# The attention stage's list of operations written anew, its last output tiles in single banks, and the next weight sum's load behind it

## The chip, the core and the metric

The kernel runs on one core of a Trainium2 chip. The metric is the time of one execution in microseconds of the device: the median of three runs is 1532.93 us (1531.55, 1532.93 and 1534.12).

The core has these engines: PE (matrix products), PEld (its weight loads, which lie beside the products), DVE, ACT and POOL (elementwise work), and SP, which mainly issues transfers. Each goes through its own list of instructions in order and waits on semaphores for the others. PE's accumulators lie in PSUM, in eight banks.

## The reference, cut to what matters

One inference step of a decoder with two layers, for 512 prompt tokens and 8 sample tokens that share the weights. The change lies in the second layer's attention (16 heads of 64, 4 key heads, a window of 128 tokens, a sink logit for each head) and ends where that layer's second feed-forward begins:

```python
q = _rope((h @ w_q[j]).reshape(B, T, N_KV_HEADS, GROUP, HEAD_DIM), pos)
out = _window_attention(q, kk, vv, wb, pos0, attn_sinks[j]) @ w_o[j]
x = x + out
x = x + 0.5 * _swiglu(_rmsnorm(x, norm_g[l, 2]), ...)

# in _window_attention, per block of 128 queries and its 256 keys
s = q @ k * HEAD_DIM ** -0.5;  s = where(mask, s, -inf)
m = max(max(s), sink);  p = exp(s - m)
denom = sum(p) + exp(sink - m)
out = (p / denom) @ v
```

## The kernel before, in words

Everything runs with the model dimension (1024, as 8 tiles of 128) on the partitions and the 520 tokens along the free axis, in two halves of 260 columns. Each float32 operand is split into a high and a low part, and a product is three matmuls (high by high, low by high, high by low): one k step of one output tile is 6 matmuls of 260 columns (`mm`, L883). For weights the high part is an ACT copy (`wh`, L450, or L421 where the queue of weights makes it) and the low part a DVE subtraction (`wl`, L454 or L425), for a chunk of 4 k steps at a time. `wh` and `wl` have six buffers.

The attention stage is all of `yoco_step` from L1937 to the next feed-forward. PSUM is there two "duos" of two banks, for products that are 520 columns wide and for scores, and four single banks, for transposes and values. The stages of a query tile t (two heads) are: eight query steps on PE (`q_step`), an ACT copy out of PSUM (`q_evac`, L1964, `qraw`); transfers that gather the rotary rows of a group of tiles (`q_gather`, L1972; the groups are tiles 0 and 1, 2 and 3, 4 to 7), four DVE passes that rotate the group (`q_turn`, L1978 to L1981), transfers back (`q_back`, L1986); the high part on ACT (L1990, `xh`) and the low part on DVE (L1993, `xl`). A `Unit` (t, h) is then two blocks of queries of these two heads: scores on PE (L2023), a DVE pass that scales, masks and takes the minimum (`masked`, L2042, one for each block and head), the exponential on ACT (`exps`, L2059), reciprocal (L2063) and scaling by it on DVE, ACT or POOL (`scale`, L2070), transposes on PE (L2081), their split on ACT and DVE (L2086, L2091), values on PE (L2108), the copy out (L2117). The samples have small operations of their own. From `oT`, split again (`o_high`, `o_low`), come 64 output steps (`o_step`, L883 too): n under 32 are the first half of the heads for each of 8 output tiles, n from 32 the second; `o_add` (L2251) adds a tile to x on DVE. For each finished x tile, ACT and DVE make the next feed-forward's input (`x_high` L2255, `x_low` L2259) and the sum of squares (`x_square` L2265, `x_sum` L2272, `acc`).

What sets the order: the string `PLAN` is a list of some 770 operations, a letter and a number each, and

```python
for step in PLAN.split():
    steps[step[0]](int(step[1:]))
```

issues them one by one. `later` keeps each engine's instructions in that order. In the list q, o, S, T and V are the products, e the copy out of a query tile, a and g its gathers, r a rotation, I and J transfers back, z and y the split of q, X, E, R, C/c/p the softmax (scaling on DVE, ACT, POOL), t and u the split of the transposes, w and W a weight chunk's high and low part, l a chunk's load.

The first 24 query steps (tiles 0 to 2) are not in the list before: a loop issues them, with the weight parts that the queue of weights gives (`W.get`, `W.prefetch`), the sums of squares' ten one-column products (L823) and the norms of `rstd_tok` and `rstd_samples` behind tile 0. Ahead of the loop stands an activation `warm` (L2129) whose only use is to load ACT's table for the exponential. The next feed-forward's first summed weight block `S` is a load on SP (L623) and an adding transfer on POOL (L627), which stand, in the order before, in the middle of the attention stage.

Of the kernel before, what the change touches and what calls it, by code (L numbers as in the profile page):

```python
# [61 lines left out]
N2 q24 N0 N1 q25 q26 z0 q27 z1 y0 q28 w11 S0 W11 S1 X0 q29 X1 E0 X2 q30 X3 q31 y1 S2 e3 S3 X4 a3 g3 q32 X5 E4  # L62
q33 X6 E1 X7 E5 q34 E6 q35 r1 E2 q40 w12 E7 q36 E3 q41 q42 R0 R1 I2 J2 c2 C4 J3 q37 W12 p7 w13 l0 c6 q43 p3 c1
c0 q38 w14 I3 q44 w15 z2 T0 q45 y2 q39 W13 q46 e4 C5 q47 S4 e5 S5 X8 S6 X9 E8 X10 S7 t0 X11 E9 T1 w16 T2 W14
N3 k2 q48 t1 X12 g4 E10 W15 q49 E11 X13 q50 E12 X14 E13 T3 X15 q51 w17 R2 W16 p8 E14 q52 C10 E15 k0 W17 q53
p11 t3 u1 q54 t2 u0 N4 c9 u2 q55 R3 S8 p12 e6 S9 X16 w18 a6 S10 X17 k3 E16 a4 X18 S11 z3 l1 X19 T4 T5 E17 q56
w19 N5 X20 g5 E18 q57 C15 p13 C14 E19 X21 q58 t5 W18 g6 q59 t4 X22 E20 a5 q60 R4 E21 u3 p18 E22 q61 X23 y3 p19
q62 E23 u5 c16 q63 k1 C17 u4 T6 R5 e7 T7 C21 C22 t6 V4 a7 N6 g7 T8 S12 u6 t8 p20 S13 X24 V5 X25 p23 E24 X26
E25 V0 u8 t7 V1 r2 E26 V2 v4 v0 V3 v1 v5 T9 v2 10 X27 t9 I4 J4 S14 v3 J5 N7 u9 S15 I5 h0 J6 11 X28 I6 J7 E27
T10 u7 I7 L0 E28 T11 b0 t10 12 R6 X29 p26 V8 z4 X30 V9 E29 y4 N9 k5 t11 13 X31 k4 E30 S18 p24 u11 z6 S19 u10  # L70
k7 E31 S16 k6 X36 c25 S17 p27 v8 R7 16 X37 z5 17 b1 p28 v9 X38 V10 z7 b3 H0 p31 E36 T12 T13 y5 t12 V11 t13 N8
X32 p29 u12 E37 14 X39 15 v10 p30 V6 E38 b2 u13 v11 Q0 T14 E39 X33 V7 X34 t14 R9 E32 20 X35 T15 p36 E33 S20 B0
v6 S21 p37 x0 X40 S22 u14 v7 S23 p38 E34 D0 V12 t15 X41 T18 p39 y6 E35 30 V13 t18 d0 u15 N10 40 v12 R8 41 u18
E40 p33 V14 v13 X42 p34 h1 X43 T19 E41 V15 y7 p35 E42 X44 42 t19 X45 43 p32 v14 S24 E43 f0 N11 S25 v15 u19 E44
44 X46 T16 T17 R10 t16 X47 45 p42 E45 u16 46 t17 X48 V18 N12 X49 c41 p43 c40 u17 V19 E46 X50 E47 T20 X51 47
E48 R11 T21 H1 v18 p44 l2 S26 t21 f1 S27 c45 p46 u21 S28 t20 s0 S29 E49 u20 p47 X52 h2 V16 T22 X53 E50 V20 G0
s1 X54 v19 V17 X55 E51 H2 V21 h3 G1 H3 s2 T23 o0 G2 N14 X56 s3 N13 t23 X57 o1 v20 G3 X58 E52 o2 X59 E53 R12 o3
j16 p48 E54 E55 o8 p49 O0 w20 o9 p50 R13 W19 t22 o10 c55 C51 l3 p53 j17 E56 o11 W20 E57 p52 o12 h4 u22 E58 u23
o13 w21 O2 o14 T24 o15 T25 O3 S30 N15 t25 S31 c54 X60 o4 W21 E60 o5 j21 t24 w22 X61 o6 u24 E61 u25 V22 E59 X62
T26 W22 E62 o7 X63 t26 V23 w23 u26 o20 w24 R14 O1 w25 T27 C56 o21 v22 C57 t27 o24 E63 o25 R15 u27 p61 o26 W23  # L80
o27 p59 j23 l4 W24 o22 w26 p58 H4 V26 p60 o23 T28 V24 O5 t28 V25 c63 C62 w27 O6 V27 h5 u28 o16 W25 v26 H5 T30
v27 o17 W26 t30 T31 v24 u30 T29 v25 o18 s4 t31 s5 o19 h6 t29 o28 H6 O4 o29 s6 w28 u29 o30 u31 V30 G6 o31 V31
O7 V28 G5 j30 V29 G4 j31 o32 v28 o36 v29 h7 o37 H7 o33 s7 o34 G7 W27 o35 l5 o38 O8 o39 P0 o40 Y0 o41 O9 o42
W28 P1 o44 w29 w30 o43 W29 w31 o45 O10 A0 o46 Y1 o47 W30 P2 o48 A1 Y2 o49 A2 W31 w32 o50 O11 l6 w33 o51 M0 P3
o52 A3 O12 o53 Y3 o56 M1 P4 o54 w34 Y4 A4 o55 o57 O13 o58 M2 A5 o59 M3 o60 M4 o61 M5 o62 W32 o63 O14 W33 A6
O15 P5 W34 w35 Y5 A7 M6 w36 P6 M7 Y6 P7 Y7 W35 W36
# [439 lines left out]
def yoco_step(ctx, tc, ins, outs):  # L526
# [429 lines left out]
    class Hidden(list):  # L956


        def __init__(self, tags):
            self.tags = tags  # L960
# [977 lines left out]
    with tc.tile_pool(name="at", bufs=2, reuse_waits="tile") as at:  # L1938
# [190 lines left out]
        later(S.activation(warm, ones[:, 0:1], AF.Exp))  # L2129

        first = W.ng
        W.ca, W.stop = 0, first + 2 * KT - 1
        o_chunk = W.items[first + 2 * KT][0]
        for t in range(3):
            for k in range(KT):
                if k % 4 == 0:
                    W.get()
                    W.prefetch()
                q_step(KT * t + k)
                if k == 3 and t == 1:  # L2140
                    seq(V.tensor_scalar(nr8, r_tok[:, :NB], -0.125, None, op0=ALU.mult))
                    rstd_samples()
                    rs8 = at.tile([P, NS], F32, name="rs8", bufs=1)
                    seq(V.tensor_scalar(rs8, R[:, SP:], 0.125, None, op0=ALU.mult))
                if k == 3 and t == 2:
                    q_turn(0)
                    for i in range(4):
                        q_back(i // 2, i % 2)
# [90 lines left out]

        def o_step(n):  # L2240
# [356 lines left out]
```

## Time and profile before

| | us |
|---|---|
| median of the three runs | 1532.93 |
| the profiled execution, its own time | 1534.7 |
| its span | 1532.8 |
| from ACT's table load, at the first query tile's end, to the score step S4 | 1042.80 to 1082.64 |
| from S4 to the first output step o0 | 1082.64 to 1140.37 |
| from the last query step q63 to o0 (part of the above) | 1099.58 to 1140.37 |
| from o0 to the last output step | 1140.37 to 1194.30 |

An engine's busy share over the whole span tells little here, since the change touches only the 170 us in the table, and the shares differ from stage to stage. A stage is read by the busy time in its stretch, by what PE waited for in it, and by the clock that PE was granted (PEclk, 1.00 is 2.4 GHz, 0.50 is 1.2 GHz).

### The profile page before, as it was taken

What the parts mean: (1) busy time and instruction counts of PE and PEld (TensorE: products, weight loads), DVE (VectorE), ACT (ScalarE), POOL (GpSimd) and SP (SyncE); (2) the same over time, 40 slices, a digit from 0 to 9 for tenths busy, and PEclk for the clock granted to TensorE, in tenths of its full rate; (3) what the DMA queues carried; (4) which work ended last, traced back from release to release, by engine and by line L of the source; (5) the groups of instructions that cost most, each with busy time, mean ns of one, the idle gap of its engine ahead of it and who ended that gap; (6) DMA issues with size and microseconds to landing.
All of it is one profiled execution on the core that took longest, in us unless ns stands there. A gap on an engine that the chain in (4) does not pass through costs nothing. (4 is left out here: it accounts for less than half of the span.)

```text
span 1532.8 us, 34975 instructions
## 1 busy us (share of the span) xinstructions
PE 1506.4 (98%) x13350; PEld 1493.4 (97%) x13350; DVE 1379.3 (90%) x2792; ACT 992.8 (65%) x2024; POOL 308.3 (20%) x346
## 2 busy tenths in 40 slices
PE   9999999999999999999999999999999999999997
PEld 9999999999999999999999999998989999999997
DVE  6999999879999999888999999885787999999976
ACT  6765765657775765656765665663886666666655
POOL 1122222001122222101322222101471122222200
PEclk9999999999999999999999999998999999999999
DMA  9589999754598999745899999762332489999941
GB/s 240 121 192 207 182 204 202 181 161 125 126 202 195 188 200 199 171 133 129 191 196 202 188 201 207 164 179 60 74 91 75 106 184 199 191 195 199 200 129 57
DMA packets 418837, 254.64 MB, mean 166 GB/s; under 512 B 13134, under 2 KB 399174, under 8 KB 418628
## 3 DMA queue, kind: packets, MB, share of 16 engines
q1 hardware_dynamic: 339390, 187.30, 44.4%
q0 software_dynamic: 75520, 60.00, 28.3%
q10 hardware_dynamic: 3758, 5.09, 1.1%
q8 instruction: 105, 1.72, 0.5%
q14 instruction: 64, 0.52, 0.1%
HBM read 218.07 MB, written 6.11 MB: 146 GB/s over the span
## 5 line engine op out<-in xcount | busy, mean ns | idle before, releaser
L450 ACT ACTIVATE wh<-raw 128x512 fp32r<-128x512 f32 (+1 forms) x718 | 441.6, 624 | 186.5 <-PE ps L913 105.1
L454 DVE TENSOR_TENSOR wl<-raw,wh 128x512 fp32r<-128x512 f32 (+1 forms) x718 | 481.4, 680 | 30.0 <-ACT wh L450 28.7
L913 PE MATMUL ps<-th,wh 128*128 128x260 f32 x1216 | 334.7, 275 | 2.5 <-DVE sb L1219 2.4
L913 PE MATMUL ps<-tl,wh 128*128 128x260 f32 x1216 | 334.4, 275 | 0.0
L913 PE MATMUL ps<-th,wl 128*128 128x260 f32 x1216 | 334.4, 275 | 0.0
L913 PE MATMUL ps<-xh,wh 128*128 128x260 f32 x896 | 246.8, 275 | 0.7 <-ACT ps L1193 0.5
L913 PE MATMUL ps<-xl,wh 128*128 128x260 f32 x896 | 246.6, 275 | 0.0
L913 PE MATMUL ps<-xh,wl 128*128 128x260 f32 x896 | 246.4, 275 | 0.0
L913 PEld LDWEIGHTS ps<-th,wh 128*128 128x128 f32 x1216 | 231.0, 190 | 3.1 <-DVE sb L1219 2.8
L913 PEld LDWEIGHTS ps<-th,wl 128*128 128x128 f32 x1216 | 231.0, 190 | 0.0
L913 PEld LDWEIGHTS ps<-tl,wh 128*128 128x128 f32 x1216 | 231.0, 190 | 0.0
L627 POOL DMA_DIRECT2D S<-in_ffn_w_up_dram x76 | 100.3, 1326 | 419.6 <-DMA S<-in_ffn_w_up_dram 106.4
L913 PE MATMUL ps<-hh,wh 128*128 128x260 f32 x656 | 181.1, 276 | 1.0 <-ACT ps L1258 0.4
L913 PE MATMUL ps<-hl,wh 128*128 128x260 f32 x656 | 181.1, 276 | 0.3 <-DVE hl L602 0.3
L913 PE MATMUL ps<-hh,wl 128*128 128x260 f32 x656 | 180.4, 275 | 0.0
L350 POOL DMA_DIRECT2D raw<-raw x108 | 95.7, 886 | 384.7 <-DVE wl L454 65.5
L913 PEld LDWEIGHTS ps<-xh,wh 128*128 128x128 f32 x896 | 170.2, 190 | 1.4 <-ACT ps L1258 0.7
L913 PEld LDWEIGHTS ps<-xl,wh 128*128 128x128 f32 x896 | 170.2, 190 | 0.3 <-DVE xl L602 0.2
L913 PEld LDWEIGHTS ps<-xh,wl 128*128 128x128 f32 x896 | 170.2, 190 | 0.0
L913 PEld LDWEIGHTS ps<-hh,wh 128*128 128x128 f32 x656 | 124.6, 190 | 2.1 <-ACT ps L1258 2.1
L913 PEld LDWEIGHTS ps<-hl,wh 128*128 128x128 f32 x656 | 124.6, 190 | 1.1 <-DVE hl L602 0.5
L913 PEld LDWEIGHTS ps<-hh,wl 128*128 128x128 f32 x656 | 124.6, 190 | 0.0
(373 smaller groups left out, 3666.9 us busy)
## 6 DMA issues: line engine op xcount, KB each, us to landing
raw<-in_ffn_w_gate_dram SPq DMA_DIRECT2D x87, 512.0 KB, 4.6
raw<-in_ffn_w_up_dram SPq DMA_DIRECT2D x87, 512.0 KB, 6.1
raw<-in_ffn_w_down_dram SPq DMA_DIRECT2D x128, 256.0 KB, 5.4
raw<-raw POOLq DMA_DIRECT2D x108, 256.0 KB, 4.4
S<-in_ffn_w_up_dram SPq DMA_DIRECT2D x76, 256.0 KB, 4.2
S<-in_ffn_w_up_dram POOLq DMA_DIRECT2D x76, 256.0 KB, 5.5
raw<-in_ffn_w_down_dram SPq DMA_DIRECT2D x16, 768.0 KB, 4.7
S<-in_ffn_w_down_dram SPq DMA_DIRECT2D x32, 256.0 KB, 3.4
```

Source lines behind the costliest of these rows:

```text
L350: G.dma_start(blk(raw, 2, 1), blk(raw, 1, 1), accum_op=ALU.add)
L450: self.pin(self.nc.scalar.activation(views[0], src, AF.Copy))
L454: self.pin(self.nc.vector.tensor_tensor(l, src, h.bitcast(F32), op=ALU.subtract))
L627: return [ld(lambda t: t, a), lambda t: nc.gpsimd.dma_start(t, b, accum_op=ALU.add)]
L913: T.matmul(bank[:, :H], a[:, kk, :], two(b), start=(not more and kk == 0 and i == 0), stop=(kk == 3 and i == 2), skip_group_check=more,)
```

## The change

The list is written anew (796 operations). It begins at q0: the loop ahead of it is gone, and so are the activation `warm` there and the queue's own weight parts. New letters issue what the loop did: U (`rstd_tok`), Z (`rstd_samples` and the scale of the samples), F (the scale of the prompt's scores), i (an `Exp` activation on one column, now behind q62). Tiles 2 and 3 are interwoven (q20, q24 to q29, q21 to q23, q30, q31), and the first scores S0 follow q31. Weight parts, softmax operations and output steps stand in other places all along; in the stretch from q63 to o0 POOL has 23 of the scalings by the reciprocal, 22 before.

The output tiles 6 and 7 of the second half take two single banks each, no duo, and have two additions of 260 columns in place of one of 520. The first `S` block is prepared behind the list.

```diff
 PLAN = """
-N2 q24 N0 N1 q25 q26 z0 q27 z1 y0 q28 w11 S0 W11 S1 X0 q29 X1 E0 X2 q30 X3 q31 y1 S2 e3 S3 X4 a3 g3 q32 X5 E4
...
+q0 N0 q1 q2 q3 q4 q5 q6 w6 W6 q7 e0 w10 W10 U0 q8 q9 q10 q11 q12 q13 Z0 w7 q14 q15 N1 w5 q16 g0 q17 q18 q19 a0
+e1 w8 W5 q20 q24 q25 W8 q26 q27 W7 q28 q29 w15 g1 a1 r0 I0 J0 z0 y0 q21 q22 q23 e2 q30 q31 e3 S0 F0 I1 w9 S1
...
         ordered[0], W.pin = True, later
-        later(S.activation(warm, ones[:, 0:1], AF.Exp))
 
         first = W.ng
-        W.ca, W.stop = 0, first + 2 * KT - 1
+        assert W.ns == W.nh == first + 5
         o_chunk = W.items[first + 2 * KT][0]
-        for t in range(3):
-            for k in range(KT):
-                if k % 4 == 0:
-                    W.get()
-                    W.prefetch()
-                q_step(KT * t + k)
...
-            q_evac(t)
-            q_gather(t, 0)
-            q_gather(t, 1)
-            if t == 0:
-                rstd_tok()
...
+        class Singles:
...
+            def __init__(self):
+                self.banks = single(), single()
...
-                parts[half, m] = duo()
+                parts[half, m] = Singles() if half and m > 5 else duo()
...
         def o_add(n):
             half, m = n // KT, n % KT
-            later(V.tensor_tensor(halves(x[m]), outs(parts.pop((half, m))), halves(x[m]), op=ALU.add))
+            banks = parts.pop((half, m))
+            if half and m > 5:
+                for hf, b in enumerate(banks.banks):
+                    xh = back(hcols(x[m], hf))
+                    later(V.tensor_tensor(xh, out(b), xh, op=ALU.add))
+            else:
+                later(V.tensor_tensor(halves(x[m]), outs(banks), halves(x[m]), op=ALU.add))
...
         steps = {
             "q": q_step,
+            "i": alone(lambda: later(S.activation(warm, ones[:, 0:1], AF.Exp))),
+            "U": alone(rstd_tok),
+            "F": alone(q_scales),
+            "Z": alone(sample_scales),
...
         W.ns = W.nh = W.ng + 5
+        W.prepare(W.items[W.next_sum()][0])
         psum(4, 0)
```

How the order changes at three places. In the rows the first number is the line in the kernel (after, lines stand two to five further down), then the operation, out<-in and the output's size.

ACT from the first query tile on, before (`raw` are loaded query weights, `qraw` the tiles' copies, `R` the samples' norm):

```order
L2129 ACT_TABLE_LOAD
L2129 ACTIVATE warm<-ones 128x1
L421 ACTIVATE wh<-raw_15360 128x512 x2
L1964 COPY qraw<-ps_15671 128x520
L421 ACTIVATE wh<-raw_15360 128x512
L854 COPY R<-ps_15729 128x8
L421 ACTIVATE wh<-raw_15483 128x512
L1964 COPY qraw<-ps_15752 128x520
```

ACT from the same place, after:

```order
L452 ACTIVATE wh<-raw_15360 128x512
L1966 COPY qraw<-ps_15671 128x520
L452 ACTIVATE wh<-raw_15483 128x512
L856 COPY R<-ps_15732 128x8
L452 ACTIVATE wh<-raw_15360 128x512 x2
L1966 COPY qraw<-ps_15751 128x520
L452 ACTIVATE wh<-raw_15483 128x512
L452 ACTIVATE wh<-raw_15608 128x512
L1992 ACTIVATE xh<-qraw 128x512
L1966 COPY qraw<-ps_15811 128x520
L1966 COPY qraw<-ps_15851 128x520
L452 ACTIVATE wh<-raw_15483 128x512
```

The table load, `warm` and one `wh` no longer stand ahead of the first tile's copy. After, the table load stands right behind the last row shown, ahead of the first exponential, and the first query split `xh` stands ahead of the copies of tiles 2 and 3.

POOL in the middle of the stretch from q63 to o0, before (`qz` are the samples' queries, `vc` their values, `sm` and `den` the softmax and its sums):

```order
L2070 TENSOR_SCALAR sm<-sm,den 128x128
L1998 COPY qz_15661<-qraw 64x8 x4
L2070 TENSOR_SCALAR sm<-sm,den 128x256 x3
L627 DMA S<-in_ffn_w_up_dram 128x4x128
L2032 COPY sm<-nsinks 128x4
L2070 TENSOR_SCALAR sm<-sm,den 128x256 x2
L2281 DMA vc<-v_new 1x16x128
L2070 TENSOR_SCALAR sm<-sm,den 128x256 x4
```

POOL's last rows in the stage, after:

```order
L2072 TENSOR_SCALAR sm<-sm,den 128x256 x6
L2072 TENSOR_SCALAR sm<-sm,den 128x128 x2
L2034 COPY sm<-nsinks 128x4 x2
L2072 TENSOR_SCALAR sm<-sm,den 128x256
L2034 COPY sm<-nsinks 128x4
L2072 TENSOR_SCALAR sm<-sm,den 128x256 x5
L629 DMA S<-in_ffn_w_up_dram 128x4x128
L352 DMA raw_18068<-raw_18068 128x512
```

The adding transfer of `S` left its place among the scalings and stands behind the last of them.

DVE at the end of the stage, before (`x_87` and `x_88` are x tiles 6 and 7):

```order
L2251 TENSOR_TENSOR x_87<-ps_17802,x_87 128x520
L454 TENSOR_TENSOR wl<-raw_17411,wh 128x512
L2251 TENSOR_TENSOR x_88<-ps_17855,x_88 128x520
L454 TENSOR_TENSOR wl<-raw_17411,wh 128x512
L2272 TENSOR_TENSOR acc<-acc,sq 128x520
L2259 SCALAR_TENSOR_TENSOR xl<-x_87,gT,xh 128x520
L2259 SCALAR_TENSOR_TENSOR xl<-x_88,gT,xh 128x520
L2272 TENSOR_TENSOR acc<-acc,sq 128x520 x2
```

DVE at the same place, after:

```order
L2254 TENSOR_TENSOR x_87<-pv_17832,x_87 128x260
L2254 TENSOR_TENSOR x_87<-pv_17833,x_87 128x260
L2264 SCALAR_TENSOR_TENSOR xl<-x_86,gT,xh 128x520
L2277 TENSOR_TENSOR acc<-acc,sq 128x520
L2254 TENSOR_TENSOR x_88<-pv_17869,x_88 128x260
L2254 TENSOR_TENSOR x_88<-pv_17870,x_88 128x260
L2264 SCALAR_TENSOR_TENSOR xl<-x_87,gT,xh 128x520
L456 TENSOR_TENSOR wl<-raw_17556,wh 128x512
L2277 TENSOR_TENSOR acc<-acc,sq 128x520
L2264 SCALAR_TENSOR_TENSOR xl<-x_88,gT,xh 128x520
```

Between the last addition to x and the end of `acc` stood six passes, and now three.

## Rows read from the trace of the kernel before

**Rows 1.** The page's busy times of the whole span, by engine.

```profile
PE 1506.4 (98%) x13350; PEld 1493.4 (97%) x13350; DVE 1379.3 (90%) x2792; ACT 992.8 (65%) x2024; POOL 308.3 (20%) x346
```

**Rows 2.** Stretches: us, busy of PE, PEld, DVE, ACT, POOL, PEclk, DMA, GB/s.

```profile
1047.31:1050.72 3.41, 3.41 (x18) 3.41 (x17) 1.45 (x7) 0.35 (x2) 0.00 (x0) 0.50 0.04 12
1064.37:1071.20 6.83, 6.64 (x38) 6.19 (x40) 3.15 (x11) 1.61 (x5) 1.41 (x5) 0.50 0.04 10
...
1082.64:1140.37 57.73, 53.49 (x515) 49.90 (x515) 49.59 (x172) 49.24 (x156) 38.48 (x64) 1.00 0.33 73
1099.58:1140.37 40.79, 36.75 (x354) 34.00 (x353) 34.48 (x122) 34.61 (x109) 28.34 (x45) 1.00 0.30 70
1140.37:1194.30 53.93, 53.57 (x482) 52.95 (x480) 42.77 (x94) 34.13 (x85) 9.43 (x12) 1.00 0.34 85
```

**Rows 3.** PE's waits in 1040 to 1240: total us, times, longest.

```profile
PE pv L2081 <- POOL sm L2070: 1.8, 1, 1.8
PE ps L2023 <- ACT xh L1990: 1.8, 1, 1.8
...
PE ps L883 <- ACT qraw L1964: 0.9, 1, 0.9
...
PE ps L823 <- DVE acc L2272: 0.5, 1, 0.5
...
PE ps L2023 <- DVE xl L1993: 0.4, 1, 0.4
```

**Rows 4.** Timeline of ACT from 1042: start, us, what, [idle before <-releaser].

```profile
1042.80 1.28 ACT L2129 ACT_TABLE_LOAD   x1 [0.35 <-issue]
1044.10 0.20 ACT L2129 ACTIVATE warm<-ones 128x1 f32<-128x1 f32 x1
1044.20 1.13 ACT L421 ACTIVATE wh<-raw 128x512 fp32r<-128x512 f32 x2
1045.24 0.57 ACT L1964 COPY qraw<-ps 128x520 f32<-128x520 f32 x1
```

**Rows 5.** Timeline of PE at the same place.

```profile
1043.83 1.17 PE L823 MATMUL ps<-ones,acc 128*128 128x1 f32 x10
1045.87 0.49 PE L883 MATMUL ps<-hh,wh 128*128 128x260 f32 x2 [0.86 <-ACT qraw L1964]
```

**Rows 6.** Timelines of ACT and DVE, tile 1's copy to the first split.

```profile
1053.40 0.59 ACT L1964 COPY qraw<-ps 128x520 f32<-128x520 f32 x1 [2.33 <-PE ps L883]
...
1063.15 1.23 ACT L1990 ACTIVATE xh<-qraw 128x512 fp32r<-128x512 f32 x2 [3.80 <-DMA qraw<-qG]
...
1057.96 0.73 DVE L1978 STREAM_SHUFFLE rp<-qG 64x520 f32<-64x520 f32 x1
```

**Rows 7.** Timeline of PE at the first scores.

```profile
1063.83 0.33 PE L2023 MATMUL ps<-tl,xh 64*128 64x128 f32 x2 [1.76 <-ACT xh L1990]
```

**Rows 8.** Chain of work that ended last, 1130 to 1150: start, us, what.

```profile
1135.94 1.60 PE ps L2023 x24
...
1138.50 1.68 PE pv L2108 x15
...
1140.62 7.37 PE ps L883 x66
```

**Rows 9.** Groups by form, 1042 to 1212: busy, mean ns of one, idle before.

```profile
L2070 POOL TENSOR_SCALAR sm<-sm,den 128x256 f32<-128x256 f32 x33 | 34.3, 1112 | 12.2 <-DVE den L2063 11.9
L2042 DVE CUSTOM_DVE_ANT_0 sm<-ps,cst,nsinks 128x256 f32<-128x256 f32 x48 | 24.6, 535 | 4.3 <-PE ps L2023 4.0
...
L454 DVE TENSOR_TENSOR wl<-raw,wh 128x512 fp32r<-128x512 f32 x31 | 21.2, 688 | 1.4 <-ACT wh L450 1.3
```

**Rows 10.** Timelines of POOL and PE around the S transfer.

```profile
1110.26 0.93 POOL L2070 TENSOR_SCALAR sm<-sm,den 128x256 f32<-128x256 f32 x1
...
1118.45 1.38 POOL L627 DMA_DIRECT2D S<-in_ffn_w_up_dram  x1 [0.83 <-PE pv L2168]
...
1121.00 0.55 PE L2081 MATMUL pv<-ident,sm 128*128 128x128 f32 x3 [1.82 <-POOL sm L2070]
```

More of the change, by code (lines that the diff above doesn't have):

```diff
@@ L67 @@
[L67 to L71, printed above, removed]
@@ L82 @@
[L82 to L86, printed above, removed]
+q0 N0 q1 q2 q3 q4 q5 q6 w6 W6 q7 e0 w10 W10 U0 q8 q9 q10 q11 q12 q13 Z0 w7 q14 q15 N1 w5 q16 g0 q17 q18 q19 a0
@@ new lines @@
+w18 t4 q51 q52 a5 L0 p12 u4 X17 E16 q53 q54 q55 E18 E17 e6 T5 S10 C14 S11 w17 q56 q57 t5 u5 q58 q59 q60 N5 u3
+q61 q62 i0 q63 w19 g6 g5 X20 E20 X23 E23 X22 W17 g4 Q0 E19 R4 p18 c16 T6 T7 X21 E21 y3 a6 E22 R5 C21 C22 S12
+C17 e7 u2 T8 t6 S13 g7 u6 p20 V0 W18 t8 V1 v0 V4 V5 t7 X24 a7 N6 X25 X27 u8 v1 p23 v5 v4 E24 E27 T10 r2 J4 J5
+p19 w23 S14 J6 12 13 b1 t10 V2 V3 u10 v2 W19 T9 t9 S15 X26 v3 u7 I6 T11 E26 V6 t11 u9 I4 E25 J7 R6 X28 h0 N9
+V8 V9 N7 X29 v9 E28 u11 z4 10 11 b0 I7 V7 X30 c25 X31 V10 y4 v6 E29 E30 I5 z5 y5 E31 V11 R7 p24 T12 t12 u12 v7
@@ new lines @@
+o17 o18 w30 p60 T30 W21 C57 T31 t31 o19 O3 t30 C56 u31 u26 o28 o29 T28 t28 u28 T29 o30 t29 w24 u29 V26 o31 O4
+V27 u30 V30 o20 o21 o22 W28 W30 v26 l4 V28 V31 v27 v25 o23 h6 H6 V29 s5 G5 W24 O7 O5 o32 o33 w25 j30 W25 s6
+o36 o37 j31 w27 W27 v29 v28 h7 G6 H7 s7 G7 o34 o35 o38 O8 o39 O9 P0 Y0 o40 o41 A0 M0 A1 M1 w31 o42 W31 l5 o43
+O10 P1 Y1 w35 W35 o44 o45 A2 M2 P2 Y2 o46 o47 O11 w36 W36 o48 o49 o50 o51 w29 W29 O12 P3 Y3 A3 M3 A4 M4 P4 w33
+Y4 o52 o53 o54 o55 O13 W33 w32 W32 o56 P5 Y5 o57 o58 o59 O14 A5 P6 M5 o60 o61 Y6 o62 l6 o63 O15 A6 M6 w34 W34
@@ L87 @@
+P7 Y7 A7 M7
 """
@@ L2128, in yoco_step, with q_scales, sample_scales @@
         ordered[0], W.pin = True, later
-        later(S.activation(warm, ones[:, 0:1], AF.Exp))
         first = W.ng
-        W.ca, W.stop = 0, first + 2 * KT - 1
+        assert W.ns == W.nh == first + 5
         o_chunk = W.items[first + 2 * KT][0]
-        for t in range(3):
-            for k in range(KT):
-                if k % 4 == 0:
-                    W.get()
-                    W.prefetch()
-                q_step(KT * t + k)
[L2140 to L2148, printed above, removed]
-            q_evac(t)
-            q_gather(t, 0)
-            q_gather(t, 1)
-            if t == 0:
-                rstd_tok()
+        rs8 = at.tile([P, NS], F32, name="rs8", bufs=1)
+        def q_scales():
+            later(V.tensor_scalar(nr8, r_tok[:, :NB], -0.125, None, op0=ALU.mult))
+        def sample_scales():
+            rstd_samples()
+            later(V.tensor_scalar(rs8, R[:, SP:], 0.125, None, op0=ALU.mult))
         prT = at.tile([P, P], F32, name="prT", bufs=1)
@@ L2238, in yoco_step, with __getitem__ @@
         parts = {}
+        class Singles:
+            def __init__(self):
+                self.banks = single(), single()
+            def __getitem__(self, at):
+                return self.banks[at[1]][:, at[2]]
         def o_step(n):
```

28 lines of the change are left out of this document (14 added, 14 removed).

## The prediction

> **What bounds the kernel now.** The first view is the page's busy times: PE is busy for 1506.4 of 1532.8 us [rows 1]. PE sets the time, so I look only for what the change does to PE's idle time and to its clock. The second view is the clock by stretch. PE is granted 1.00 throughout the stage except in two stretches of 3.41 and 6.83 us, where it gets 0.50 [rows 2]. In the first PE is busy all the time, in the second for 6.64 us: half of that work's time is the clock's, 3.41 / 2 = 1.71 and 6.64 / 2 = 3.32 us. The third view is PE's waits, which name the releaser [rows 3]. They lie at three places:
>
> - 0.86 us behind the first query tile. PE has done the ten one-column products (1.17 us) and waits for the bank that ACT's copy frees [rows 5]. That copy stands behind the table load (1.28), `warm` and two `wh` (1.13), and starts only at 1045.24 [rows 4].
> - 1.76 + 0.40 us at the first scores, whose wait ends at 1063.83 [rows 3, 7].
> - In the stretch from q63 to o0, 40.79 - 36.75 = 4.04 us, the largest single one 1.82 us, for a scaling on POOL [rows 2, 3, 10].
>
> Both slow stretches begin right behind such a place: the first 1.4 us after the 0.86 us wait, the second 0.5 us after the wait for the first scores. No fall follows the 1.82 us wait, since the middle shows 1.00 [rows 2]. So I price the first two places with their clock, and the third by its wait alone. From o0 on PE has 53.93 - 53.57 = 0.36 us idle, and 0.46 us wait for `acc` at the end [rows 2, 3].
>
> **Front: the loop's part of the list.** Ahead of tile 0's copy one `wh` is left, 1.13 / 2 = 0.57 us; the table load, `warm` and the other `wh` are gone (1.28 + 0.20 + 0.57 = 2.05 us). The copy starts about 1043.8, when the tile's last product ends, and is done (0.57) at about 1044.4, while the ten one-column products last until 1045.0 [rows 4, 5]. Nothing is left to wait for: **-0.86 us**. With PE busy there I expect no fall of the clock behind it: **-1.71**. The table load isn't gone, it now stands ahead of the first exponential: its 1.28 us lie on ACT while PE is at the scores and tile 4's steps, with nothing of PE behind it but the first transposes.
>
> A page of the Trainium skill speaks against this placing: "ScalarE: Activation LUTs", section "What ACT_TABLE_LOAD costs", has a load followed by a drain, together near 2.66 us. Here the next activation starts at 1044.10, 1.30 us after the load's start, so no drain shows [rows 4], and the row decides. By the page the first transposes would be later by some 0.5 us, and the gain smaller by that much, as an estimate.
>
> **First scores.** From tile 1's copy to the first split the chain (gather transfers, four rotation passes, transfers back) took from 1053.99, the copy's end, to 1063.15: 9.16 us [rows 6]. In the new list PE runs through tile 1 without the wait and the slow stretch. Before, tile 1 was done at about 1053.3; less 0.86 and 1.71 that is about 1050.7. One `wh` (0.63) stands ahead of its copy (0.59), so the copy ends at 1051.9 and the split starts at 1061.1. Ahead of S0 stand three more query steps than before (it follows q31, and followed q28), of 6 x 0.112 = 0.67 us each [rows 8]. PE's last query step ahead of S0 ended at 1063.83 - 1.76 = 1062.07 [rows 7]; less 2.57, plus 2.0, that is about 1061.5. The split's high part is there at 1061.7, but S0 needs a duo, and that is freed by tile 2's copy, which stands behind the split on ACT: 1061.1 + 0.6 + 0.6 = 1062.3. So a wait of about 0.9 us stays where 2.16 stood: **-1.26**. At 0.9 us I expect the clock to hold. The evidence is thin: it held through 1.82 us in the middle and fell after 0.86 with one-column products ahead of it and after 2.16. I take it as held, **-3.32**; the other end, that it falls as before, is a rival. Front: -0.86 - 1.71 - 1.26 - 3.32 = -7.15 us.
>
> **Middle, from S4 to o0.** The new list brings S4 earlier, with 30.0 us of PE work ahead of it and not 35.3 (steps of 0.67, scores of 6 x 0.067 = 0.40, transposes of 4 x 0.11, values of 6 x 0.112, counted along both lists with the durations of [rows 8]). So more lies between S4 and o0. Counted in the same way, before: PE 49.9, DVE 50.5, ACT 46.2; after: PE 51.4, DVE 50.0, ACT 48.2. The total of PE's work is the same in both. From q63 to o0 alone, before: PE 34.0, DVE 35.2, POOL 26.2 and the S transfer; after: PE 30.3, DVE 37.3, POOL 28.1. DVE's main passes there are the 0.535 us mask pass, 32 in both, and the 0.69 us weight part, no longer 3 of them but none [rows 9]. So the middle isn't thinner than before; DVE stands closer to PE at its end. The 1.38 us S transfer on POOL leaves the middle. It stood ahead of two scalings whose last released PE after 1.82 us [rows 10]; with it gone POOL's queue is shorter by 1.38, but 23 scalings stand there where 22 did, each 0.93 alone and 1.11 in the mean [rows 9, 10]. Going along the new list I find these places where PE reaches an operation before its input: the samples' back-and-forth (0.65, 0.3), a score step whose bank waits for a mask pass (1.1), a value step (0.7), o0 on the last split (0.9), a transpose (0.5), some 4.2 us, and with the small ones of DVE's end 5.2. Before it was 57.73 - 53.49 = 4.24 [rows 2]. So **+1.0**; the ends are -4.2 (all of it hidden) and +7 (DVE at its share of before), both rivals.
>
> **From o0 on.** 56.6 us of PE work stand here, 52.9 before; the work is moved, not added. It was 99% busy [rows 2]. Some units' transposes now stand among the output steps with less DVE slack: **+0.5**, ends 0 and 2. The two single banks spare a wait for a duo at o56, of which the rows show none, and cost two more DVE instructions: nothing either way. Behind the last addition only three passes stand before `acc` is whole, six before; at 0.7 us each that is 2.1 us, more than the 0.46 us wait for `acc` [rows 3]: **-0.46**. The S transfer at its new place hides behind the feed-forward's first two weight chunks, since that block isn't split until some 15 us later; if not, it costs its 1.38.
>
> **Sum.** -7.15 + 1.0 + 0.5 - 0.46 = -6.1 us. The profiled execution took 1534.7, which becomes 1528.6; it lay 1.8 above the median, so against the median 1532.93 the forecast is **1526.8**.
>
> **Rivals.** (a) Every wait of the middle goes as well: the list is made so that PE always has a query or output step between a unit's steps. For it: the middle's idle is spread over small hand-overs. Against: DVE has 50 us of work in 55 there. Gain 7.15 + 4.04 + 0.46 = 11.65, 1521.3.
>
> (b) The front doesn't do what the order says: the wait at S0 stays at about 2.2 us, because the transfers of the rotation are as long and PE arrives earlier, and the clock falls behind it as before. Left of the gain: 0.86 + 1.71 + 0.46 - 1.5 = 1.5 us, 1531.4. For it: the first scores hang on a 9.16 us chain that the change doesn't shorten.
>
> (c) DVE or POOL paces the end of the middle. DVE's 37.3 us from q63 to o0 at the share it had, 34.48 / 40.79 = 0.845, take 44.1 us, and my forecast has 38.1 for it (30.3 us of PE work as the rows time it, x 36.75 / 34.0, + 5.2 and the like): 6.0 us more, 1532.8. For it: the mask pass and the scaling are what PE waited for before. "SBUF — State Buffer" of the Trainium skill, section "SBUF: two separate sides", has GpSimd and VectorE share ports under an exclusive lock, which would bring this case about. The rows show POOL's scaling at 0.93 alone and 1.11 in the mean [rows 9, 10], a small part of what a lock held for each DVE pass would cost; by that page, with a lock held for a 0.69 pass each, the 23 scalings would take 37 us as an estimate, and the change would gain some 3 us less.
>
> (d) The other side: PE's waits in the middle come dense enough for the clock to fall there. 4 us of further waits, and half of some 34 us of PE's work at 0.50, another 8 (as a stretch at 0.50 costs half of its busy time [rows 2]): -6.1 + 12 = +5.9, 1538.8. It decides at the first stretch of the middle with a clock under 1.00. Against it: 4.04 us of idle in 40.79 left the clock at 1.00 [rows 2].
>
> **How the numbers follow.** The forecast 0.62, (a) 0.13, (b) 0.10, (c) 0.08, (d) 0.07. A measurement of this kernel tells some 0.2% from no change, 3.1 us, so faster begins under 1529.9 and slower over 1536.0. Faster: nearly all of the forecast (0.59), (a) and a bit of (b) and (c): 0.75. Same: the rest of the forecast, of (b) and most of (c): 0.16. Slower: (d) and the upper end of (c): 0.09. The range leaves out (d), the far half of (a) and the upper half of (c): 1521.0 to 1532.8.
>
> **What would show it.** In the changed kernel: no PE wait for `qraw` behind the ten one-column products; no clock of 0.50 in the first 30 us of attention; a wait of about 0.9 us, not 2, at the first scores; S4 at about 1070.2 (1082.64 less 7.15 less the 5.3 us of work that moved behind it); o0 near 1130.8, for the middle's 51.4 x 53.49 / 49.9 + 5.2 = 60.3 us and a bit; the last output step's end near 1188.9, no wait for `acc`. A slow stretch behind S0 would make the front wrong, PE idle of over 8 us between S4 and o0 the middle.

## The result, and the profile after

The changed kernel takes 1536.49 us in the median of 15 runs (1535.42 to 1537.87); the kernel before, beside it, 1532.68 (1529.85 to 1535.98). The ratio is 1.0024, 95% interval 1.0016 to 1.0032: slower, by some 3.8 us, where 6.1 us faster was forecast. The profiled execution took 1536.74 us, near the median; that of before, 1534.7, lay 2 us above its own.

The stretches of the changed kernel, from the first query tile's end to S4, S4 to o0, q63 to o0, o0 to the last output step, and two stretches at a low clock (columns as in [rows 2]):

```profile
1044.02:1070.68 26.66, 26.16 (x240) 25.49 (x239) 14.81 (x46) 13.06 (x29) 4.38 (x12) 1.00 0.34 83
1070.68:1139.46 68.78, 64.74 (x527) 59.11 (x527) 53.11 (x174) 51.44 (x160) 35.08 (x64) 0.88 0.31 72
1093.83:1139.46 45.63, 41.89 (x316) 37.47 (x314) 33.89 (x116) 32.23 (x101) 23.39 (x40) 0.81 0.25 55
1139.46:1197.47 58.01, 57.95 (x521) 56.93 (x520) 47.79 (x106) 39.87 (x99) 10.82 (x16) 1.00 0.22 60
...
1113.12:1123.36 10.24, 9.56 (x50) 9.11 (x52) 8.09 (x31) 8.71 (x29) 6.99 (x9) 0.50 0.01 2
1130.18:1137.01 6.83, 6.83 (x36) 5.71 (x36) 5.44 (x22) 3.83 (x13) 2.33 (x3) 0.50 0.70 157
```

The front is at 1.00 throughout, where [rows 2] had two stretches at 0.50. The middle, at 1.00 in [rows 2], now has two stretches at 0.50, 10.24 + 6.83 = 17.07 us together, of which half is lost: 8.5 us (8.2, if the 0.68 us for which PE still waited in the first are left out). PE's waits in 1035 to 1240, against [rows 3]:

```profile
PE pv L2158 <- issue: 3.5, 1, 3.5
PE ps L885 <- ACT R L870: 0.9, 1, 0.9
PE ps L2025 <- DVE nm L2044: 0.5, 1, 0.5
PE pv L2083 <- DVE sm L2072: 0.3, 1, 0.3
PE pv L2083 <- DVE xl L2093: 0.2, 1, 0.2
```

The waits for the tile's copy, for the first scores, for POOL's scaling and for `acc` are gone. One new wait of 3.5 us stands at L2158, a product of the samples' scores. Timelines of the first places, ACT and PE, against [rows 4, 5, 7]:

```profile
1043.93 0.63 ACT L452 ACTIVATE wh<-raw 128x512 fp32r<-128x512 f32 x1 [0.26 <-issue]
1045.25 0.59 ACT L1966 COPY qraw<-ps 128x520 f32<-128x520 f32 x1 [0.69 <-PE ps L885]
...
1064.06 1.28 ACT L2061 ACT_TABLE_LOAD   x1 [0.27 <-DVE nm L2044]
1065.36 0.41 ACT L2061 ACTIVATE sm<-sm,nm 128x129 f32<-128x129 f32 x1
...
1045.05 1.17 PE L825 MATMUL ps<-ones,acc 128*128 128x1 f32 x10
1046.09 0.47 PE L885 MATMUL ps<-hh,wh 128*128 128x260 f32 x2
...
1062.57 0.33 PE L2025 MATMUL ps<-tl,xh 64*128 64x128 f32 x2
```

The copy is done at 1045.84, the one-column products end at 1046.09, and PE goes on. S0 has no wait. Now the new wait, in the chain of work that ended last from 1103 to 1116, and on SP, ACT and PE:

```profile
1103.97 0.32 POOL sm L2034 x2
1104.28 0.20 issue
1104.48 0.47 POOL qraw L1988
1104.96 6.94 DMA qraw<-qG
...
1112.44 0.20 POOL qz L2000
1112.63 1.17 issue
1113.80 0.99 PE pv L2158 x4
```

```profile
1101.30 2.40 SPq L1988 DMA_DIRECT2D qraw<-qG  x4
1103.76 27.28 SPq L625 DMA_DIRECT2D raw<-in_w_o_dram  x4
...
1111.92 0.63 ACT L1992 ACTIVATE xh<-qraw 128x512 fp32r<-128x512 f32 x1 [2.83 <-DMA qraw<-qG]
...
1113.34 0.37 ACT L2119 COPY oT<-pv 64x256 f32<-64x256 f32 x1
...
1113.80 0.99 PE L2158 MATMUL pv<-qz,kc 128*128 128x8 f32 x4 [3.51 <-issue]
```

In POOL's list two of the four transfers back of the last rotation (I7, I5) stand behind two sink copies (L2034), which wait for PE's transposes. So they are issued from 1104.48 on, just after SP has begun to issue the next output weights' loads at 1103.76, and the last of them lands 6.94 us after it is issued. POOL's sample copies (`qz`) and ACT's split of tile 5 (L1992) both wait for it until 1111.9. PE's product needs `qz` (1112.63) and a PSUM bank that ACT frees with the copy at 1113.34, queued behind that split. It starts 1.17 us after `qz` is there: the bank came last. The clock falls at 1113.12, inside this wait, when PE had been idle for 2.8 us.

The second stretch at 0.50 has no wait ahead of it. What stands there, up to 0.4 us ahead of the fall at 1130.18, are transposes and 24 of the samples' value products (8 columns each) in one row; the kernel before has at most 8 of them in a row:

```profile
1127.01 2.74 PE L2204 MATMUL pv<-prT,vc 128*128 128x8 f32 x24
```

A stretch at 0.50 loses half its length. The profiled time, the loss in the attention stage, and the rest:

| profile | us | lost to the clock | rest |
|---|---|---|---|
| before | 1534.70 | 5.1 | 1529.6 |
| changed | 1536.74 | 8.5 | 1528.2 |

By these two profiles the change gains 1.4 us without the clock. The forecast without its two clock terms was -6.1 + 5.0 = -1.1.

Two profiles are two executions. But every execution on record has its mean granted clock: 0.99273 in the mean of the 15 of the changed kernel, 0.99549 in that of the 133 of the kernel before that were measured beside the experiments. The difference is 0.00276, and 0.00276 x 1534 = 4.2 us, where the median rose by 3.8. PE is busy for 98% of the span, so a clock lost is a time lost, nearly: the slowdown is clock, and what the change gains without it can't be told from nothing.

### The profile page after: what moved, and what is told of

Read it like the earlier page. It is cut to its first block, busy times and chain, and to the rows that moved or that the text cites. A ratio compares the mean times of both kernels' runs of the same rounds, so it can differ in the third digit from the quotient of the medians.

```text
span 1535.0 us, 34974 instructions
## 1 busy us (share of the span) xinstructions
PE 1511.8 (98%) x13350; PEld 1496.5 (97%) x13350; DVE 1380.3 (90%) x2794; ACT 993.9 (65%) x2024; POOL 304.4 (20%) x346
## 3 DMA queue, kind: packets, MB, share of 16 engines
q8 instruction: 105, 1.72, 0.5%
## 5 line engine op out<-in xcount | busy, mean ns | idle before, releaser
L456 DVE TENSOR_TENSOR wl<-raw,wh 128x512 fp32r<-128x512 f32 (+1 forms) x724 | 488.1, 685 | 32.5 <-ACT wh L452 31.0
```

The source lines that it names most:

```text
L456: self.pin(self.nc.vector.tensor_tensor(l, src, h.bitcast(F32), op=ALU.subtract))
```

## The experiments

Theory T: the late transfer, the wait and what the clock does behind it. Rival U: DVE and ACT pace the middle, and the transfer is only the last of several late inputs. Four runs on this. (Of an edit to the list only the operations around a move are shown, and not every helper operation that moves along.)

**The two transfers moved** ahead of the sink copies, in the changed list:

```diff
-u9 I4 E25
-b0 I7 V7
-E30 I5 z5
+u9 I4 I7 I5 E25
+b0 V7
+E30 z5
```

> The changed kernel, with the two transfers back I7 and I5 on POOL moved from behind the sink copies N9 and N7 to right behind I4. Theory T: in the changed kernel PE waits 3.51 us at 1113.80 for sample queries whose last transfer back was issued at 1104.48, behind those copies and just after SP began two 256 KB loads at 1103.76, and took 6.94 us; the clock falls to 0.50 behind the wait, from 1113.6 to 1123.4. With the transfers ahead of the loads they land in about 2 us, the wait goes (3.5) and the first slow stretch with it (4.8): 1536.5 becomes 1528.2; if the second slow stretch (1130 to 1137, 3.3 us) was an aftermath of the first, 1524.9. Rival U: the middle of the new list is paced by DVE and ACT, the transfer is only the last of several late inputs, and the wait moves to the next one: 1534 to 1536.5.

**The load later**, by the low part that frees its buffer:

```diff
-v2 W19 T9
-z5 y5 E31
+v2 T9
+z5 y5 W19 E31
```

> The changed kernel, with the low part W19 of a weight chunk moved on DVE to behind y5. The third output weight load takes that chunk's buffer, so it then starts only after tile 5's transfer back has landed; the transfers and POOL's order stay. Theory T: the loads are what makes the transfer slow; it lands about 2 us after its issue at 1104.5, as in the kernel before, and the time is that of the run with the transfers moved, 1528 (1525 if the second slow stretch goes too). Rival P: POOL's place alone makes it late, the loads don't matter: 1536, no change. Rival U: 1534 to 1536.

The medians are 1531.83 and 1532.11 us, ratio to before 0.9994 (0.9984 to 1.0005) and 0.9997 (0.9988 to 1.0006). POOL and SP in the first, then in the second, and the first's stretches at 0.50:

```profile
1100.69 1.99 POOL L1988 DMA_DIRECT2D qraw<-qG  x4 [2.81 <-DVE sT L2163]
1103.13 0.32 POOL L2034 COPY sm<-nsinks 128x4 f32<-128x4 f32 x2 [0.45 <-PE pv L2083]
...
1110.03 0.58 PE L2158 MATMUL pv<-qz,kc 128*128 128x8 f32 x4 [0.58 <-POOL qz L2000]
```

```profile
1104.94 0.96 POOL L1988 DMA_DIRECT2D qraw<-qG  x2 [0.20 <-issue]
...
1109.05 2.40 POOL L2000 COPY qz<-qraw 64x8 f32<-64x8 f32 x6
...
1111.42 14.14 SPq L625 DMA_DIRECT2D raw<-in_w_o_dram  x3
```

```profile
1113.33:1116.74 3.41, 3.41 (x22) 3.19 (x20) 2.77 (x14) 3.41 (x16) 2.06 (x3) 0.50 0.03 5
1123.57:1130.39 6.82, 6.82 (x36) 5.90 (x34) 5.61 (x23) 3.91 (x13) 2.37 (x4) 0.50 0.75 156
```

Either edit takes the wait from 3.5 to 0.6 and 0.8 us. In the second the transfers are issued as late as in the changed kernel (1104.94), and only the load is out of their way. So it takes both: the place on POOL's list and the load that goes ahead. And either edit takes the whole slowdown away: against the kernel before, 1.0024 has become 0.9994 and 0.9997, no difference. What stays away is the forecast gain. (The loads are two of 512 KB; the expectation's 256 is a slip.) T holds against U for the wait; for the clock T was right in part only. Of 8.3 us 4.7 came back. A stretch of 3.41 us stayed where 10.24 was, the second stayed as it was (6.82), and 5.1 us are lost to the clock in the stage.

**Spreading the samples' value products** on top of the first edit:

```diff
-40 42 N10 t15 u15 T18 R8
-43 41 f0 t19 X42 E42 u19 R10 44 45 h2 47
-V14 S24 T16
-c41 S25 X46
+40 N10 t15 u15 T18 42 R8
+43 t19 X42 E42 u19 R10 41 f0 44 S24 45 S25 h2 47
+V14 T16
+c41 X46
```

> As the run with the two transfers moved, and the samples' value products (40 to 47, 8 columns each) spread: 42 behind the transposes T18, 41 later, and the score steps S24 and S25 between 44, 45 and 47. Theory T: the second slow stretch of the changed kernel (clock 0.50 from 1130.3 to 1136.9, with no wait ahead of it) comes from 5 us of such narrow products and transposes one behind the other; spread, it goes: 3.3 us under the run with the transfers alone, 1525. Rival A: it is an aftermath of the first slow stretch or of the transposes, and the spreading does nothing: the same as the run with the transfers alone, within 1 us.

1532.13 us: no gain, as rival A said. The profile has the same 5.1 us lost, in one stretch from 1121 to 1132, and two more waits, of 0.7 us at a score step and of 1.0 us.

**The table load back in front** of the changed kernel:

```diff
-q6 w6 W6 q7 e0 w10 W10
-q62 i0 q63
+q6 i0 w6 w10 W6 q7 e0 W10
+q62 q63
```

> The changed kernel with the exponential's warm activation (i0) back ahead of the first query tile's copy, with two weight parts behind it as in the kernel before, so that the table load of 1.28 us stands there. Theory T: PE waits 0.9 us for the copy again, and the clock falls behind the ten one-column products: +0.9 +1.7, 1539.1; if the clock doesn't fall, 1537.4. Rival: the wait of before came from the order of the queue's weight parts and not from the table load: no change, 1536.5.

1536.04 us, ratio to before 1.0020 (1.0010 to 1.0030): no change against the changed kernel. The profile shows the wait for the copy again, but 0.5 us and no fall of the clock behind it. The 1.71 us of the forecast's second term don't follow from the table load alone.

Next, theory T2: the samples' narrow products (8 columns), put one behind the other, bring the clock down; the list before spreads them. Rival A2: the middle's clock falls whatever the order. Two merged lists (the new one up to a point, then what is left in the old order) and two edits of the kernel before:

```diff
 q39 a3 g2
-E4 X5 R0 e4
+N2 W11 X5 E4
```

> The new list up to g2 (tile 4's third step on), and from there the operations of the old list that are left, in the old list's order; the single banks and the place of the S load stay as changed. Theory T2 (after the run with the transfers moved, in which the wait of 3.5 us became 0.6 but slow stretches of 4 and 7 us stayed): the front of the new list gains its 7.2 us, and what takes it back are the samples' narrow products, which the new list puts one behind the other and the old one spreads between wide products. So here the front gains and the middle shows no clock under 1.00: 1533.0 - 7.2 = 1525.8. Rival A2: the clock falls in the middle because PE comes there with DVE and ACT further behind, whatever the order: slow stretches of some 7 to 10 us stay, 1529.5 to 1531.

```diff
 T10 r2
-J4 J5 p19 w23
+p19 X26 E25 E26
```

> The new list up to r2 (the last rotation), and from there the operations that are left in the old list's order; the single banks and the place of the S load stay as changed. T2: as with the front alone, within 1.5 us (1524.5 to 1527), no clock under 1.00 in the middle. Rival A2: as the run with the two transfers moved, 1531.8, with a slow stretch. Rival V: the part of the new list from tile 4's steps to r2 has a cost of its own: 2 us or more above the run with the front alone.

1531.99 us (ratio 0.9997, 0.9985 to 1.0008) and 1536.83 (1.0034, 1.0022 to 1.0045). Both lists have waits of their own where they meet, one from each:

```profile
PE ps L2024 <- ACT qraw L1965: 1.6, 1, 1.6
```

```profile
PE pv L2157 <- ACT oT L2118: 2.5, 1, 2.5
```

Behind the first the clock fell for 3.41 us, behind the second for 13.65. T2 had 1525.8 and at most 1527, so it missed both; the second is 4.8 us above the first, as rival V had it, but with its own wait in it. So these two say little on what the parts are worth. They show that a wait in this part of the program can cost more than itself; it needn't, since the wait of 1.7 to 1.8 us for POOL's scaling has no fall right behind it in three of the four profiles that show it (the kernel before, the two runs that follow), and has one in the fourth, the second profile of the kernel before.

**The kernel before with its value products in one row**:

```diff
-40 v12 R8 41 u18
-42 t19 X45 43
-44 X46
-47 45 p42
-46 t17
-47 E48
-f0 N11
-f1 S27
+v12 R8 u18
+40 41 42 t19 X45 43 44 45 46 47
+f0 f1 N11
```

> The kernel before, with the samples' value products 40, 41 and 44 to 47 moved to 42 and 43, so that the eight groups of 8-column products follow each other (f1 behind f0). Work, transfers and all else stay. T2: the clock falls to 0.50 behind them for some 7 us, which costs 3.3 us: 1536.3. Rival A2: the order of the narrow products doesn't matter while PE has no wait: 1533, no change.

1534.86 us, ratio 1.0021 (1.0010 to 1.0032). Timeline of PE, and the stretch behind it:

```profile
1123.39 3.64 PE L2214 MATMUL pv<-prT,vc 128*128 128x8 f32 x32
1126.96 0.33 PE L2023 MATMUL ps<-tl,xh 64*128 64x128 f32 x2
```

```profile
1127.24:1130.65 3.41, 3.41 (x24) 3.19 (x23) 3.26 (x15) 1.86 (x6) 1.68 (x3) 0.54 0.56 148
```

PE was busy without a break, and the clock fell behind the 32 narrow products: no wait is needed. The median rose by 2.8 us, T2 said 3.3. The mean granted clock says the same of all executions: 0.99383 in the 12 of this run, 0.99582 in the 33 of the kernel before beside them, a difference of 3.0 us. In the profile the stretch is half as long as expected, and there is a second of 3.41 us from 1199 on, behind the wait for `acc` and its one-column products.

**The kernel before without the early table load**:

```diff
-        later(S.activation(warm, ones[:, 0:1], AF.Exp))
```

> The kernel before without the warm activation at the start of attention, so that the table load stands ahead of the first exponential. Two weight parts still stand ahead of tile 0's copy. The prediction's first two terms: the wait of 0.86 goes and the slow stretch behind it (1.71): 1533.0 - 2.6 = 1530.4. Rival: the run with the table load put back in the changed kernel showed a wait of 0.5 and no fall, so the fall isn't the wait's: 1532.1 if only the wait goes, with the clock at 0.50 after the one-column products all the same.

1530.41 us, ratio 0.9991 (0.9980 to 1.0003); its profile took 1528.90, with no stretch under 1.00 in the stage. The wait of 0.86 is gone. The time is the forecast's 1530.4, but the gain of some 1.6 us is not told apart from none.

**Wide products between the narrow ones**, on top of the two transfers moved:

```diff
-S16 H1 k7 k5 k6 14
-S17 E37 b2
-T14 u13 X32 V12 V13 S20
-41 f0 t19
-h2 47 46
-V14 S24 T16
+S16 S17 H1 k7 k5 k6 V12 14
+E37 V13 b2
+T14 X32 S20
+p33 V14 42 T19 X44 X45 N11 V15 43 41 f0 t19
+h2 S24 47 46
+p35 S25 T17
```

> As the run with the two transfers moved, with wide products put between the samples' narrow ones: S17 and V12 ahead of 14, V13 behind 15, V14 and V15 between 40, 42 and 43, S24 between 45 and 47, S25 ahead of T17 (and the splits and copies out that these need). The same work. T2: the slow stretches of 4 and 7 us (5.1 us lost in that run's profile) go, and the wait of 0.6 for the sample queries is covered: 1531.8 - 5.1 - 0.6 = 1526.1, faster than both kernels. Rival A2: the clock falls in the middle whatever stands between: 1531 to 1532. A part of it, should one stretch stay: 1528.5.

1536.33 us: 4.5 us slower than without. Its profile has 13.64 and 6.82 us at 0.50. The groups 16, 17 and 15 still stood together (12 narrow products, 1.61 us), and V12 to V15, put further up, no longer stood behind them. Moving what is there made it worse; T2 in its simple form, that spreading is enough, found no support.

**The kernel before once more**, unchanged:

> The kernel before once more, for a second profile. The prediction took the two slow stretches of its one profile (1047 to 1051, 1064 to 1071; 5.0 us) as what every execution loses. If so, they are there again. In the profile of the kernel before with only its sample products bunched, they were not, while its median is higher: then the stretches come in some executions and not in others, this profile shows other ones or none, and the prediction's 5.0 us were too much for the median.

1530.70 us. PE's timeline, and the one stretch at a low clock:

```profile
1115.71 0.60 PE L2081 MATMUL pv<-ident,sm 128*128 128x128 f32 x3 [1.77 <-POOL sm L2070]
```

```profile
1115.92:1119.33 3.41, 3.41 (x22) 3.08 (x20) 0.66 (x2) 2.39 (x10) 3.41 (x6) 0.52 0.49 61
```

It lost 1.7 us to the clock, and not at the two places of [rows 2] but behind the wait for POOL's scaling, of which the prediction said that no fall follows it. The rest, 1529.0, is that of the first profile within 0.6 us. The Trainium skill, "TensorE: Matmul & The Clock Gate", section "Part 1: The HAM clock gate", says of the clock's rise at a kernel's start that its point varies from run to run of the same kernel. These two profiles show the like of its falls in the middle of one.

**The small parts undone** in the changed kernel:

```diff
-                parts[half, m] = Singles() if half and m > 5 else duo()
+                parts[half, m] = duo()
...
-            if half and m > 5:
+            if isinstance(banks, Singles):
...
-        W.prepare(W.items[W.next_sum()][0])
```

> The changed kernel with its two small parts undone: the last two output tiles in duos with one addition of 520 columns each, and no preparing of the S block behind the list. The prediction gave the single banks nothing either way and the S transfer's place a hidden 1.38 us: if both hold, 1536.5, no change. If the single banks or the order at the end of DVE were worth the 0.46 us wait for acc, 1537 with that wait and, at the fourteen one-column products, a slow stretch (1.7 us more). If the S transfer on POOL stands ahead of what PE waits for, more than 1537.

1536.05 us (ratio 1.0021): no change, and no wait for `acc` either. So what took that wait away is the order of DVE's last passes, not the single banks.

Theory T3: the new list does its wide work (query steps, values) early, and what is left beside the narrow products of the middle is too little; adding wide work should keep the clock up. In three runs, wide products that no output needs were added:

```diff
+        def wide(to, n):
+            for _ in range(n):
+                later(T.matmul(to[:, 256:512], kk[0][0][:, :P], kk[0][0][:, :256], start=True, stop=True))
...
+            if g:
+                wide(bank["s", n], 4)
...
+            wide(bank["v", b // 4], 4)
```

> As the run with the two transfers moved, and with work added that no output needs: 4 wide products (128x256 out of 128 rows, into unused columns of the same bank) behind each of the last four groups of sample scores and behind each of the eight groups of sample values, 48 in all, some 0.11 us each, 5.3 us of PE time. Theory T3: what brings the clock down in the middle is how little wide work PE has there beside its narrow products (the samples', the transposes), since the new list does wide work (query steps, values) earlier; moving what is there only moves the hole. Then the added work keeps the clock at 1.00 and pays for itself: 1531.8, less some 6 us that the clock takes in the median, plus 5.3: 1531, with no slow stretch in the profile. Rival W: the clock falls behind PE's waits or at these places whatever PE does: slow stretches stay and the work is added, 1537.

> As the run before it with 2 added wide products at each of the twelve places, 2.6 us. T3: if that is enough, no slow stretch, 1531.8 - 6 + 2.6 = 1528.4, under both kernels; if not, one stretch stays, 1530 to 1532. Rival W: 1534.4.

> The changed kernel itself (the transfers late as they are), with the same 4 added wide products at each of the twelve places, and 26 more (2.9 us) ahead of the sample scores that wait 3.5 us for the late transfer, so that PE is busy through most of the wait. T3: the clock stays at 1.00 although the inputs are as late as before: 1536.5 - 8.2 + 5.3 = 1533.6 at most, less where the added work lies in the wait. Rival W: the late transfer itself is the cost, filled or not: 1536.5 + 5 = 1541.

The first took 1532.73 us (ratio 0.9993, 0.9982 to 1.0004). Its stretch from q63's end to behind o0, in one row:

```profile
1093.00:1140.00 47.00, 46.04 (x411) 41.98 (x410) 37.82 (x129) 36.42 (x115) 27.42 (x44) 1.00 0.25 53
```

The 48 products cost more than expected, 0.14 us each (four from 1129.36 to 1129.92 in the third run), 6.7 us together. The median rose by 0.9 against the run with the transfers moved, so 5.8 us of clock came back by the medians; by the mean granted clock (0.99509 in the 11 executions there, 0.99745 in the 11 here) it is 3.6. The profile shows 1.00 in the whole attention stage, where that run has two stretches at 0.50. No input moved and PE waits no less: the same 0.6 us for the sample queries, and 0.96 us idle in these 47 us against 0.80. So it is shown that in this list the clock stays up when wide products are added between the narrow ones, with the same waits. That the change thinned the middle by doing wide work early fits this, but no run puts that work back alone, and the run with wide products moved between the narrow ones shows that the amount is not all. Half as much was not enough: 1533.38 us, a little above the range that T3 gave it, with one stretch of about 7 us left in the stage, at the sample scores; behind the 24 value products none is left. In the third the 26 products meant for the wait need the same PSUM bank that comes late, so they waited too and then ran.

```profile
1114.79 4.89 PE L2153 MATMUL pv<-tl 128*128 128x256 f32 x26 [3.55 <-ACT oT L2119]
```

1541.37 us, rival W's number and not T3's, with 1.7 lost to the clock in the stage where the changed kernel loses 8.5. It confirms the bank as the last thing the wait was for; between T3 and W it doesn't decide, since the wait was not filled.

Last, two parts of the change alone in the kernel before, both without the early table load:

```diff
         W.ns = W.nh = W.ng + 5
+        W.prepare(W.items[W.next_sum()][0])
```

> The kernel before without the warm activation (1530.4) and with the S block prepared behind the list, the change's third part alone. The prediction gave the S transfer's 1.38 us on POOL no gain of its own, but in the kernel before it stands ahead of the scalings that release PE after 1.7 to 1.8 us. If it is what makes them late, that wait falls to some 0.4: 1530.4 - 1.4 = 1529.0. If POOL's scalings are late without it, no change: 1530.4.

```diff
-q28 w11 S0 W11 S1 X0 q29 X1 E0 X2 q30 X3 q31 y1 S2 e3
+q28 w11 W11 q29 q30 q31 S0 S1 X0 X1 E0 X2 X3 y1 S2 e3
```

> As the run before it, and the first scores S0 to S2 with their mask passes behind q31, as in the changed kernel, so that three query steps (2.0 us) more stand ahead of S0. The prediction's second term: the wait at the first scores, 1.44 us with the table load away, is covered: 1529.0 - 1.4 = 1527.6, and one place fewer where the clock can fall. Rival: with the exponentials later, tile 4's banks and the first softmax come later by the same time, and the wait turns up there: 1529.

With `S` behind: 1529.93 us, ratio 0.9984 (0.9971 to 0.9997), faster than before and than the changed kernel. Against the run without the table load alone (0.9991) the difference isn't clear of noise. The 1.8 us wait for POOL's scaling is gone from the profile, which took 1531.54 at a loss of 5.1 us to the clock in the stage and 1.7 ahead of it. The transfer cost more in its old place than its own 1.38 us: the six scalings behind it take 1.41 to 1.47 us each in the profile of the kernel before and in three more of its order, and 0.91 to 0.92 here. Before:

```profile
1119.47 2.36 POOL L2070 TENSOR_SCALAR sm<-sm,den 128x256 f32<-128x256 f32 x2
...
1121.83 4.13 POOL L2070 TENSOR_SCALAR sm<-sm,den 128x256 f32<-128x256 f32 x4
```

(A stretch of 3.41 us some 73 us after the start, far ahead of the change, is there in 8 of the 18 profiles, of kernels with the old front and the new.)

With the scores later as well: 1532.00 (1.0004, 0.9991 to 1.0016). The rival was right there:

```profile
PE ps L2023 <- ACT qraw L1964: 3.0, 1, 3.0
```

The wait at the first scores went and came back larger at the copy of a tile whose bank the next scores need. The changed kernel, in which the rest of the list was moved too, has no such wait.

## Why the prediction was wrong

Step by step, as the prediction put it:

- **The wait for the copy, -0.86**: right, in place and size.
- **The first scores, -1.26**: the direction right, the size small. There is no wait left, so 2.16 went. S4 starts at 1070.68, forecast 1070.2, in a trace in which the ten one-column products already came 1.2 us later.
- **The two slow stretches, -1.71 and -3.32**: gone in the changed kernel's profile, and in no profile of the new front (twelve) was one seen there. But they were not what every execution of the kernel before loses. Its second profile has neither. By that profile's rest (1529.0) and the first's (1529.6), the median near 1532.5 contains some 3 us of clock, at places that change (by the mean granted clocks it is about 4). A term was taken from one profile and set against a median: that is the first step that failed.
- **Middle, +1.0 for waits**: the sum came near by luck, and the mechanism was wrong. PE has 68.78 - 64.74 = 4.04 us of idle time from S4 to o0; 5.2 were forecast, 4.24 stood before. Forecast were many small hand-overs; it is one wait of 3.51. The prediction gave POOL's scalings a price and the `S` transfer its 1.38 us, and never followed the transfers back: which of POOL's entries stand ahead of them, and which load SP issues at that moment. Both stand in the order of the instructions.
- **The clock in the middle**: the step that decided. The sum has no term for it: the middle stood at 1.00, and 8.5 us were lost there. Rival (d) had it, at a chance of 0.07, with 8 us of clock. That the sizes agree is partly luck: (d) wanted PE's waits to grow by 4 us, and they didn't grow. One wait stands ahead of the first stretch, and none ahead of the second. What spoke against (d) was a single row at 1.00 [rows 2] and "no fall follows the 1.82 us wait". In the second profile one does. The counting along the list had a number that bears on it: from q63 to o0 PE's work falls from 34.0 to 30.3 us (counted once more, by two score steps, two transposes and four value steps, 4.4 us), while the narrow products of the samples stay the same and their value products come together. It was read as balance between engines, and not as thinner work for PE: "So the middle isn't thinner than before". That this thinning is what brings the clock down is argued from the runs with added products, not shown alone. (The sentence there on DVE's weight parts has them the wrong way round: the list before has none from q63 to o0, the new one three. The sum of DVE's work, 35.2 to 37.3 us, goes by the right count.)
- **From o0 on, +0.5**: PE has 0.06 us of idle time there, 0.36 before; forecast slightly too high. **acc, -0.46**: right, by the order of DVE and not by the single banks.
- **S behind the list, nothing**: right for the changed list, where undoing it with the single banks changed nothing. Alone, in the kernel before, it takes away the 1.8 us wait, which the prediction did not expect of it: it priced the transfer at its own 1.38 us, and not the 0.5 us by which each of the six scalings behind it ends later.
- **The two rules of the Trainium skill in the prediction**: the table load at 1064.06 is followed by the next activation at 1065.36, 1.30 us later, no drain here either. POOL's scalings took 952 ns in the mean, 1112 before [rows 9], beside as many DVE passes, so a lock that holds every one of them for a DVE pass doesn't show. But the means hide two things. Six of the 33 before stand behind the `S` transfer. And single scalings are held: of those before, the one from 1160.08 takes 1.72 us beside two DVE passes that subtract one SBUF tile from another (`wl` from 1159.80, `hl` from 1160.41), in the changed kernel the one from 1096.45 takes 1.36 beside such a pass (`wl`, 1096.18 to 1097.03), where most take 0.92. Beside the mask passes, which read PSUM, they take 0.92 to 0.93.

In sum: the change is slower by the late transfer, its wait and the clock behind it, since moving that transfer alone brings the time of the kernel before. And it isn't faster, even then, because the clock is lost in the middle all the same. Of the 6.1 us, 1.1 were waits and the order of work; the two profiles show 1.4 there, and all executions nothing that stands out. The other 5.0 were clock, and there the change doesn't gain them but loses 4.2 us more than the kernel before.

What stays open: what of the new order thins the middle, since no run puts the moved wide work back, and why wide products moved between the narrow ones made it worse. With 24 added products the clock still fell once, with 48 it didn't; other amounts and places were not tried. Whether the front alone gains in the median is not known either, since the merged list brought a wait of its own.

## What to carry to other kernels

Before a clock term goes into a sum, take it from more than one execution: the same kernel lost 5.1 and 1.7 us in two profiles, at different places. The mean granted clock of all executions, where it is on record, gives the size. When a list of operations is packed, count for each stretch how much wide work PE has left beside its narrow products and transposes; taking wide work out to an earlier stretch may cost the clock where it was taken from, which is what this case suggests. And of every small transfer that several engines wait for, look up what stands ahead of it in its queue and which large load starts beside it.

## What the runs showed of the hardware

A transfer of 32.5 KB took 6.94 us from its issue, beside a load in two pieces of 512 KB that SP had begun to issue 1.2 us earlier; with the load out of the way the four of that queue took 1.8 us in the median. The granted clock fell to 0.50 behind 3.64 us of 8-column products in which PE had no idle time at all, and with wide products added between such groups it stayed at 1.00 through 47 us in which PE waited as before. There 6.7 us more of PE work cost 0.9 us of time in the median. One kernel, unchanged, had stretches at 0.50 at different places in two executions.
